# Hybrid encoder step on one core: the last output pair in another order, its last product in two column halves, a shorter 1/sqrt for one column, and the final gain multiplied in ahead

## The chip, the core and the metric

The kernel runs on one core of a Trainium2 chip. The metric is the time of one execution on the device in microseconds (us), lower is better. The engines work in parallel, each on its own list of instructions in order: PE (matrix products, with PEld for the load of the stationary operand), DVE and ACT (elementwise work), POOL (a few copies and DMA issues) and SP (DMA issues). They wait for each other by semaphores. DMA queues are named after the engine that issues (SPq, ACTq, POOLq).

## The reference

One layer on 4096 prompt rows and 32 sample rows of width 1024. What this case touches is the end of it: the output projection, the residual and the last RMSNorm.

```python
def rmsnorm(x, g):
    xf = x.astype(jnp.float32)
    y = xf * lax.rsqrt(jnp.mean(xf * xf, axis=-1, keepdims=True) + EPS)
    return (y * g.astype(jnp.float32)).astype(x.dtype)
...
    h = rmsnorm(x, norm_g)
    proj = jnp.einsum('btd,de->bte', h, w_in)
    u, v, z_a, xb, z_b = jnp.split(proj, ...)
    a = u * chunk_mlp(layernorm(v, ln_v_g, ln_v_b), w_spatial, b_spatial) * jax.nn.silu(z_a)
    b = pool_mix(x_ext, pos0, w_pool, pool_scale) * jax.nn.silu(z_b)
    y = x + jnp.einsum('bte,ed->btd', jnp.concatenate([a, b], axis=-1), w_out)
...
y_prompt = rmsnorm(xp, final_g)
```

`concat(a, b)` is 2048 wide, `w_out` is 2048 x 1024, `final_g` has 1024 entries.

## The kernel before

All large products are made in float32 precision from two parts: each operand is split in a high part (rounded to the type that PE multiplies fast) and the rest, and each product is high x high, high x low and low x high, so three matmuls per 128 rows of the contraction. On top of that the products are blocked 2 x 2 by a scheme with seven products instead of eight (numbers `q` 0 to 6), whose operands are sums and differences of blocks.

The output projection works on pairs of row tiles: `OutPair(z, i)` takes rows 256 i to 256 i + 255 (tiles n = 0 and 1, 128 rows each) and one half z of the 2048 contraction rows. First all 16 pairs with z = 0 (their sums go to `part` in DRAM, or stay in SBUF for the last two), then those with z = 1, which finish the rows. The very last step of the program is pair 13 with z = 1.

One product is 4 x 3 matmuls of 128 x 128 by 128 x 512 into one PSUM bank (`multiply`, L671 to L680). Products share banks: 0, 2 and 4 one, 3 and 6 another, 1 and 5 have their own. After a product DVE adds the bank to halves of the two result tiles `y[0]`, `y[1]` (L684; which half after which product is the table in L681). Left half means columns 0 to 511. With z = 1, ACT squares each finished half and sums it over the columns into `ss` (L688, an ACTIVATE and an ACTIVATION_READ_ACCUMULATOR). Product 1 finishes the left half of tile 0, product 4 the right half of tile 1, product 5 the right half of tile 0, product 6 the left half of tile 1.

`finish` (L691) takes the two sums, divides by 1024 and adds EPS (L700, L701), makes 1/sqrt by a bit trick and three Newton steps (`rsqrt`, L82 to L91: two steps for the first guess, then three times three), multiplies the tile by that column and by the gain `f_bc` (L706, DVE) and stores it (L709). For all pairs but the last it runs after product 2 of the next pair, on both tiles, and stores over POOL's queue. In the last pair `finish(0)` is called right after product 5 and `finish(1)` after product 6 at the end of the program, each with its own 13 steps; there the scaling goes in two halves of 512 columns, and the left half is stored over SP's queue, the right one over ACT's.

The instructions of an engine are put in order by the recording layer when the program is built; `tc.keep_in_program_order` (used by the change) keeps an instruction behind those recorded before it on its engine.

Of the kernel before, what the change touches and what calls it, by code (L numbers as in the profile page):

```python
# [10 lines left out]
BF16 = mybir.dt.bfloat16  # L11
# [4 lines left out]
P = 128  # L16
D = 1024
# [18 lines left out]
def stream_step(ctx: ExitStack, tc, x_prompt, x_sample, state_pool, norm_g, w_in, ln_v_g, ln_v_b,  # L36
# [39 lines left out]
    def small(tag, n, rows=P):  # L76
        return smallp.tile([P, 8], F32, tag=tag, name=tag)[:rows, :n]
# [4 lines left out]
    def rsqrt(a, n, rows=P):  # L82

        y, t = small("rs_y", n, rows), small("rs_t", n, rows)
        nc.vector.tensor_single_scalar(t.bitcast(I32), a.bitcast(I32), 1, ALU.logical_shift_right)
        nc.vector.tensor_scalar(y.bitcast(I32), t.bitcast(I32), -1.0, float(0x5F3759DF), ALU.mult, ALU.add)
        for _ in range(3):
            nc.vector.tensor_tensor(t, y, y, ALU.mult)
            nc.vector.scalar_tensor_tensor(t, t, -0.5, a, ALU.mult, ALU.mult)
            nc.vector.scalar_tensor_tensor(y, t, 1.5, y, ALU.add, ALU.mult)  # L90
        return y  # L91

    def slot():
        return slots.tile([P, 2 * 4 * WIDE], F32R, tag="slot", name="slot")
# [525 lines left out]
    class OutPair:  # L620
# [39 lines left out]
        def begin(self, y=None):  # L660
# [7 lines left out]
                self.ss = smallp.tile([P, 2, 2], F32, tag="sq", name="sq", bufs=4)  # L668
            self.acc = {}

        def multiply(self, q):  # L671
            own = {0: 0, 1: 1, 2: 0, 3: 3, 4: 0, 5: 5, 6: 3}[q]
            if own == q:
                self.acc[own] = acc_tile()
            x, w = self.ops[q], w_slots[self.z, q]
            a, fresh = self.acc[own], own == q
            for k in range(4):
                mm(a, x[:, 0, k, :], w[:, k, 0], start=fresh and k == 0, stop=False, skip_group_check=True)  # L678
                mm(a, x[:, 0, k, :], w[:, k, 1], start=False, stop=False, skip_group_check=True)  # L679
                mm(a, x[:, 1, k, :], w[:, k, 0], start=False, stop=k == 3, skip_group_check=True)  # L680
            for n, h, bank in {0: [(0, 0, 0)], 1: [(0, 0, 1)], 2: [(1, 0, 0)], 3: [(1, 1, 3)], 4: [(0, 1, 0), (1, 1, 0)],  # L681
                               5: [(0, 1, 5)], 6: [(1, 0, 3)]}[q]:
                y = self.y[n][:, h * 512:(h + 1) * 512]
                nc.vector.tensor_tensor(y, self.acc[bank], y, ALU.add)  # L684
            if self.z and q in (1, 4, 5, 6):
                n, h = {1: (0, 0), 4: (1, 1), 5: (0, 1), 6: (1, 0)}[q]
                junk = sum_p.tile([P, 2 * 512], BF16, tag="sum", name="junk")[:, :512]
                nc.scalar.activation(junk, self.y[n][:, h * 512:(h + 1) * 512], AF.Square,  # L688
                                     accum_out=self.ss[:, n, h:h + 1])

        def finish(self, last=None):  # L691
            t0 = 2 * self.i * P
            if self.z == 0:
                for n in range(2):
                    nc.gpsimd.dma_start(part[t0 + n * P:t0 + (n + 1) * P, :], self.y[n])
                return
            tiles = (0, 1) if last is None else (last,)
            a = small("ssa", 2)
            ss, a = self.ss[:, tiles[0]:tiles[-1] + 1], a[:, :len(tiles)]
            nc.vector.tensor_tensor(a, ss[:, :, 0], ss[:, :, 1], ALU.add)  # L700
            nc.vector.tensor_scalar(a, a, 1.0 / D, EPS, ALU.mult, ALU.add)  # L701
            r = rsqrt(a, len(tiles))
            for n in tiles:
                y = self.y[n]
                for z, c in enumerate((slice(0, 512), slice(512, D)) if last is not None else (slice(0, D),)):
                    nc.vector.scalar_tensor_tensor(y[:, c], y[:, c], r[:, n - tiles[0]:n - tiles[0] + 1], f_bc[:, c],  # L706
                                                   ALU.mult, ALU.mult)
                    queue = nc.gpsimd if last is None else (nc.sync, nc.scalar)[z]
                    queue.dma_start(yp[t0 + n * P:t0 + (n + 1) * P, c], y[:, c])  # L709

    class OutSample:

# [49 lines left out]
    with ExitStack() as ph:  # L762
# [215 lines left out]
            groups += [pools[2:4]] + [[x] for x in gates + pools[4:]] + [pools[:2]]  # L978
        n_sets = len(groups)
        pairs = [[OutPair(z, i) for i in range(SEQ // (2 * P))] for z in range(2)]  # L980
        groups += [[x] for x in pairs[0][:-2]] + [pairs[0][-2:], pairs[1][-2:]] + [[x] for x in pairs[1][:-2]]
        orders = [[(g[0], q) for q in range(NQ)] if len(g) == 1 else lagged(*g) for g in groups]
        steps = [x for order in orders for x in order]
        first = {id(s): i for i, (s, q) in reversed(list(enumerate(steps))) if q == 0}
        loads = [(first[id(s)], 1, s) for g in groups for s in g]
# [78 lines left out]
    with ExitStack() as ph:  # L1064
        y_p = pool("y_p", 6, ph)
        spare_p = pool("spare_p", 2, ph)
        ps_more = pool("ps_more", 2, ph, space=bass.MemoryType.PSUM)

        def y_tile():
            return y_p.tile([P, D], F32, tag="y", name="y")  # L1070

        def more_tile():
            return ps_more.tile([P, 512], F32, tag="more", name="more")

        def spare_tile():
            return spare_p.tile([P, D], F32, tag="spare", name="spare")


        m_edge = DEC + HALO
        state = {}  # L1080

        def state_load(k):
            if k == 0:
                state["acc"] = [more_tile(), more_tile()]
            state["st"] = st = sum_p.tile([P, 512], F32R, tag="sum", name="st")[:, :P]
            nc.sync.dma_start(st.bitcast(F32), stk[:, k * P:(k + 1) * P])
            state["raw"] = raw = raw_tile()
            nc.sync.dma_start(raw, w_in[0, k * P:(k + 1) * P, 3 * D:4 * D])

        def state_split():  # L1090
            hi, lo = state["parts"] = [weight_tile().rearrange("p h k t -> p (h k t)") for _ in range(2)]
            nc.scalar.copy(hi, state["raw"])
            lo_part(lo, state["raw"], hi)

        def state_rows(k):
            accs, st, (hi, lo) = state["acc"], state["st"], state["parts"]
            for z in range(2):
                c = slice(z * 512, (z + 1) * 512)
                mm(accs[z], st, hi[:, c], start=k == 0, stop=False, skip_group_check=True)
                mm(accs[z][:m_edge], st[:, :m_edge], lo[:, c], start=False, stop=k == KT - 1, skip_group_check=True)  # L1100
            if k == KT - 1:
                low = raw_tile()
                for z in range(2):
                    c = slice(z * 512, (z + 1) * 512)
                    nc.scalar.copy(low[:m_edge, c], accs[z][64:64 + m_edge])
                    nc.vector.tensor_tensor(low[:m_edge, c], accs[z][:m_edge], low[:m_edge, c], ALU.add)
                nc.sync.dma_start(st_prompt[0, 0], low[m_edge - POOL_STATE:m_edge])
                nc.sync.dma_start(st_sample[0, 0], low[DEC - POOL_STATE:DEC])

        samples = {n_sets + 1: OutSample(0), len(groups) - 6: OutSample(1)}  # L1110
        kept, ended = [], None
        for n in range(n_sets, len(groups)):
            g, order = groups[n], orders[n]
            for s in g:
                s.begin(kept.pop(0) if kept else None)
            if g[0].z and ended is None:
                f_bc = spare_tile()
                nc.sync.dma_start(f_bc, final_g.partition_broadcast(P))
            for m, (s, q) in enumerate(order):
                at += 1  # L1120
                prepare(at + LEAD)
                if m == 0 and n in samples:
                    samples[n].load()
                k = n - n_sets - 4
                if 0 <= k < KT and m in (0, 2):
                    state_load(k) if m == 0 else state_split()
                s.multiply(q)
                if n == len(groups) - 1 and q == 5:
                    s.finish(0)
                if m == 2 and ended:  # L1130
                    for x in ended:
                        x.finish()
                if s is g[-1] and n + 1 < len(groups) and groups[n + 1][0].stage != s.stage:
                    load_out_weights(1, q)
                if 0 <= k < KT and m == 6:
                    state_rows(k)
            if n in samples:
                samples[n].multiply()
            ended = g
            if g[0].z == 0 and len(g) == 2:  # L1140
                kept, ended = [x.y for x in g], None
        ended[0].finish(1)


# [27 lines left out]
```

## Time and profile before

| | us |
|---|---|
| median of 3 runs | 2402.03 |
| the three runs | 2402.02, 2402.03, 2408.12 |
| the profiled execution, its own time | 2403.8 |
| its span in the profile | 2402.0 |
| PE busy | 2372.8 (99% of the span) |
| DVE busy | 1799.3 (75%) |
| ACT busy | 894.6 (37%) |

The span goes from the first to the last event that the profile shows. Rows of the timeline give start and duration in us, then engine, source line, operation, result and operands ("out<-in"), the shape in partitions x elements, a count where equal rows are merged, and in brackets the idle time of the engine ahead of it with what ended it. Operands are named by the program's tiles: `acc` and `more` are PSUM banks, `wop` split operands, `slot` the split weights, `spare` holds the gain, `sq` the sums of squares, `rs_t` and `rs_y` the columns of 1/sqrt, `ssa` its argument. Matmuls are pipelined, so that one starts before the one ahead has drained; their ends are modelled.

### The profile page before, as it was taken

What the parts mean: (1) busy time and instruction counts of PE and PEld (TensorE: products, weight loads), DVE (VectorE), ACT (ScalarE), POOL (GpSimd) and SP (SyncE); (2) the same over time, 40 slices, a digit from 0 to 9 for tenths busy, and PEclk for the clock granted to TensorE, in tenths of its full rate; (3) what the DMA queues carried; (4) which work ended last, traced back from release to release, by engine and by line L of the source; (5) the groups of instructions that cost most, each with busy time, mean ns of one, the idle gap of its engine ahead of it and who ended that gap; (6) DMA issues with size and microseconds to landing.
All of it is one profiled execution on the core that took longest, in us unless ns stands there. A gap on an engine that the chain in (4) does not pass through costs nothing.

```text
span 2402.0 us, 32539 instructions
## 1 busy us (share of the span) xinstructions
PE 2372.8 (99%) x11910; PEld 1987.7 (83%) x11910; DVE 1799.3 (75%) x3327; ACT 894.6 (37%) x1594; POOL 198.9 (8%) x386
## 2 busy tenths in 40 slices
PE   8999999999999999999999999999999999999998
PEld 6788887788888888888888899999978788888876
DVE  6977787866787766877668776668767777588887
ACT  5555544333433333333334333333323232233332
POOL 1000000100011000111000110112200000000000
PEclk9999999999999999999999999999999999999999
DMA  9878977422448334474334472334687776855442
GB/s 282 287 284 264 271 249 241 141 92 92 149 129 294 103 97 132 132 276 135 106 105 141 167 264 87 99 102 149 223 308 258 255 259 228 308 177 166 155 128 83
DMA packets 325241, 445.56 MB, mean 185 GB/s; under 512 B 19324, under 2 KB 248444, under 8 KB 322392
## 3 DMA queue, kind: packets, MB, share of 16 engines
q1 hardware_dynamic: 273336, 354.65, 44.8%
q0 software_dynamic: 21136, 69.29, 8.0%
q10 hardware_dynamic: 30608, 19.53, 2.9%
q8 instruction: 94, 1.54, 0.3%
q14 instruction: 67, 0.55, 0.1%
HBM read 273.75 MB, written 169.66 MB: 185 GB/s over the span
## 4 chain that ended last, share of the span: by engine, by line
PE 96%; DMA 1%; DVE 1%; ACT 0%; issue 0%; SPq 0%; DVEq 0%; ACTq 0%
PE acc L172 22%; PE acc L174 22%; PE acc L173 22%; PE acc L678 8%; PE acc L680 8%; PE acc L679 8%; PE sp L893 2%; PE tr L442 1%; PE acc L237 1%; DMA slot<-wops 1%; DMA wops<-raw 0%; DMA vt<-in_w_in_dram 0%; PE more L742 0%; PE more L741 0%; PE tr L373 0%; DVE slot L80 0%
## 5 line engine op out<-in xcount | busy, mean ns | idle before, releaser
L172 PE MATMUL acc<-slot,wop 128*128 128x512 f32 (+1 forms) x2240 | 791.9, 354 | 1.2 <-ACT t L148 1.2
L174 PE MATMUL acc<-slot,wop 128*128 128x512 f32 (+1 forms) x2240 | 784.4, 351 | 0.9 <-DVE wop L80 0.9
L173 PE MATMUL acc<-slot,wop 128*128 128x512 f32 (+1 forms) x2240 | 784.4, 350 | 0.0
L80 DVE TENSOR_TENSOR wop<-raw,wop 128x512 fp32r<-128x512 f32 x510 | 353.1, 695 | 160.2 <-ACT wop L105 140.6
L172 PEld LDWEIGHTS acc<-slot,wop 128*128 128x128 f32 x2240 | 422.5, 189 | 59.6 <-ACT t L148 1.7
L174 PEld LDWEIGHTS acc<-slot,wop 128*128 128x128 f32 x2240 | 421.7, 188 | 60.4 <-DVE wop L80 1.4
L173 PEld LDWEIGHTS acc<-slot,wop 128*128 128x128 f32 x2240 | 422.4, 189 | 57.1 <-issue 0.2
L105 ACT CAST wop<-raw 128x512 fp32r<-128x512 f32 x340 | 210.3, 621 | 404.2 <-PE acc L174 320.6
L678 PE MATMUL acc<-slot,wop 128*128 128x512 f32 x896 | 353.6, 395 | 4.7 <-DMA slot<-wops 3.6
L679 PE MATMUL acc<-slot,wop 128*128 128x512 f32 x896 | 353.5, 395 | 0.0
L680 PE MATMUL acc<-slot,wop 128*128 128x512 f32 x896 | 353.2, 395 | 0.0
L146 DVE TENSOR_TENSOR t<-acc,t 128x512 f32<-128x512 f32 (+1 forms) x320 | 186.6, 584 | 128.6 <-ACT t L155 72.0
L684 DVE TENSOR_TENSOR y<-acc,y 128x512 f32<-128x512 f32 x256 | 173.3, 687 | 99.4 <-PE acc L680 98.0
L678 PEld LDWEIGHTS acc<-slot,wop 128*128 128x128 f32 x896 | 168.7, 188 | 45.6 <-issue 4.0
L680 PEld LDWEIGHTS acc<-slot,wop 128*128 128x128 f32 x896 | 168.8, 188 | 39.7
L679 PEld LDWEIGHTS acc<-slot,wop 128*128 128x128 f32 x896 | 168.8, 188 | 39.2
L172 PE MATMUL acc<-slot,op 128*128 128x512 f32 x448 | 181.0, 405 | 0.0
L174 PE MATMUL acc<-slot,op 128*128 128x512 f32 x448 | 177.1, 396 | 0.0
L173 PE MATMUL acc<-slot,op 128*128 128x512 f32 x448 | 176.8, 395 | 0.0
L640 ACT CAST wop<-raw 128x512 fp32r<-128x512 f32 x160 | 98.1, 620 | 190.1 <-PE acc L680 178.6
L80 DVE TENSOR_TENSOR wop<-sum,wop 128x512 fp32r<-128x512 f32 x200 | 137.0, 685 | 29.0 <-ACT wop L105 23.6
L912 POOL DMA_DIRECT2D abT<-t x128 | 69.5, 543 | 871.7 <-DVE t L924 631.8
(203 smaller groups left out, 2488.8 us busy)
## 6 DMA issues: line engine op xcount, KB each, us to landing
raw<-in_w_in_dram SPq DMA_DIRECT2D x102, 512.0 KB, 4.1
xops<-op SPq DMA_DIRECT2D x72, 512.0 KB, 5.9
abT<-t POOLq DMA_DIRECT2D x128, 256.0 KB, 3.6
raw<-abT SPq DMA_DIRECT2D x64, 512.0 KB, 5.2
slot<-xops SPq DMA_DIRECT2D x30, 1024.0 KB, 10.8
slot<-wops SPq DMA_DIRECT2D x14, 2048.0 KB, 9.1
xt<-in_x_prompt_dram SPq DMA_DIRECT2D x32, 512.0 KB, 4.9
raw<-v_all SPq DMA_DIRECT2D x32, 512.0 KB, 3.5
```

Of the source, the lines that this page charges most:

```text
L80: nc.vector.tensor_tensor(out, src, hi.bitcast(F32), ALU.subtract)
L105: nc.scalar.copy(hi, src)
L146: add = lambda o, x, y: nc.vector.tensor_tensor(o, x, y, ALU.add)
L172: mm(acc, sh, mh, start=fresh and k == 0, stop=False, skip_group_check=True)
L173: mm(acc, sh, ml, start=False, stop=False, skip_group_check=True)
L174: mm(acc, sl, mh, start=False, stop=k == 3, skip_group_check=True)
L640: nc.scalar.copy(t[:, 0], src)
L678: mm(a, x[:, 0, k, :], w[:, k, 0], start=fresh and k == 0, stop=False, skip_group_check=True)
L679: mm(a, x[:, 0, k, :], w[:, k, 1], start=False, stop=False, skip_group_check=True)
L680: mm(a, x[:, 1, k, :], w[:, k, 0], start=False, stop=k == 3, skip_group_check=True)
L684: nc.vector.tensor_tensor(y, self.acc[bank], y, ALU.add)
L912: nc.gpsimd.dma_start(abT[row, :, t0:t0 + HALF], t[:, :HALF])
```

## The change

The last pair gets a class of its own, `LastPair`, with its products in the order 0, 1, 2, 3, 4, 6, 5. Product 6, now last but one, finishes tile 1. Product 5, now last, is made in two halves of 256 columns, each in a bank of its own (`more`), with an add and a square of its own.

Tile 1 is multiplied by the gain into a tile `out` as soon as its halves are finished, and so is the left half of tile 0 in place; the squares are taken before that. What is left at the end is a multiplication by the column 1/sqrt: for tile 1 one copy on ACT with a scale, 1024 wide, and one store over SP's queue; for tile 0 one copy on ACT (left half, stored over ACT's queue) and one multiplication by column and gain on DVE (right half, stored over SP's).

The 1/sqrt works on m = -(sum/1024 + EPS)/2, into which the sums are added as they come, one step each. A Newton step is then two instructions instead of three: t = y * y * m, y = (t + 1.5) * y. The constant of the first guess is changed to fit m. `finish` loses its argument and its branch for single tiles.

```diff
+    def rsqrt_steps(m):
+        y, t = small("rs_y", 1), small("rs_t", 1)
+        stt = nc.vector.scalar_tensor_tensor
+        guess = [lambda: nc.vector.tensor_single_scalar(t.bitcast(I32), m.bitcast(I32), 1, ALU.logical_shift_right),
+                 lambda: nc.vector.tensor_scalar(y.bitcast(I32), t.bitcast(I32), -1.0, float(0x9EF759DF), ALU.mult,
+                                                 ALU.add)]
+        return y, guess + 3 * [lambda: stt(t, y, y, m, ALU.mult, ALU.mult),
+                               lambda: stt(y, t, 1.5, y, ALU.add, ALU.mult)]
...
+        def product(self, q, acc, c, fresh=True):
+            x, w = self.ops[q], w_slots[self.z, q]
+            for k in range(4):
+                mm(acc, x[:, 0, k, :], w[:, k, 0, c], start=fresh and k == 0, stop=False, skip_group_check=True)
+                mm(acc, x[:, 0, k, :], w[:, k, 1, c], start=False, stop=False, skip_group_check=True)
+                mm(acc, x[:, 1, k, :], w[:, k, 0, c], start=False, stop=k == 3, skip_group_check=True)
...
+    class LastPair(OutPair):
+        ORDER = (0, 1, 2, 3, 4, 6, 5)
+        def multiply(self, q):
...
+            elif q == 1:
...
+                acc = product_tile(acc_tile)
+                tt(y0[:, lo], acc, y0[:, lo], ALU.add)
+                square(y0[:, lo], ss[:, 0, 0:1])
+            elif q == 4:
+                self.product(q, self.acc[0], lo, False)
+                for y in (y1, y0):
+                    tt(y[:, hi], self.acc[0], y[:, hi], ALU.add)
+                square(y1[:, hi], ss[:, 1, 1:2])
+                tt(y0[:, lo], y0[:, lo], f_bc[:, lo], ALU.mult)
+                tt(self.out[:, hi], y1[:, hi], f_bc[:, hi], ALU.mult)
+                for n in range(2):
+                    ts(self.m[n], ss[:, n, n:n + 1], scale, shift, ALU.mult, ALU.add)
+            elif q == 6:
+                self.product(q, self.acc[3], lo, False)
+                in_order(tt(y1[:, lo], self.acc[3], y1[:, lo], ALU.add))
+                square(y1[:, lo], ss[:, 1, 0:1])
+                in_order(tt(self.out[:, lo], y1[:, lo], f_bc[:, lo], ALU.mult))
+            else:
+                (m0, m1), t0 = self.m, 2 * self.i * P
+                sums = [ss[:, 0, 1:2], small("end2", 1)]
+                r1, steps = rsqrt_steps(m1)
+                steps.insert(0, lambda: stt(m1, ss[:, 1, 0:1], scale, m1, ALU.mult, ALU.add))
+                for n, acc_sum in enumerate(sums):
+                    c = slice(n * 256, (n + 1) * 256)
+                    acc = product_tile(more_tile, c)
+                    c = slice(512 + n * 256, 512 + (n + 1) * 256)
+                    in_order(tt(y0[:, c], acc, y0[:, c], ALU.add))
+                    square(y0[:, c], acc_sum)
+                    for _ in range(6 if n == 0 else 3):
+                        in_order(steps.pop(0)())
+                nc.scalar.activation(self.out, self.out, AF.Copy, scale=r1)
+                nc.sync.dma_start(yp[t0 + P:t0 + 2 * P, :], self.out)
+                for acc_sum in sums:
+                    in_order(stt(m0, acc_sum, scale, m0, ALU.mult, ALU.add))
+                r0, steps = rsqrt_steps(m0)
+                for step in steps:
+                    in_order(step())
+                nc.scalar.activation(y0[:, lo], y0[:, lo], AF.Copy, scale=r0)
+                stt(y0[:, hi], y0[:, hi], r0, f_bc[:, hi], ALU.mult, ALU.mult)
+                nc.sync.dma_start(yp[t0:t0 + P, hi], y0[:, hi])
+                nc.scalar.dma_start(yp[t0:t0 + P, lo], y0[:, lo])
...
+        pairs[1][-3] = LastPair(1, SEQ // (2 * P) - 3)
...
-                if n == len(groups) - 1 and q == 5:
-                    s.finish(0)
...
-        ended[0].finish(1)
```

The order of the instructions shows three places; in the rows below 20522 is `y[0]` and 20523 is `y[1]` of the last pair, and `end0`, `end1`, `end2` are the new columns for m. On DVE, from the add of product 1 to those of product 4, before:

```order
L684 TENSOR_TENSOR y_20522<-acc_20548,y_20522 128x512
L684 TENSOR_TENSOR y_20523<-acc_20531,y_20523 128x512
L684 TENSOR_TENSOR y_20523<-acc_20597,y_20523 128x512
L684 TENSOR_TENSOR y_20522<-acc_20531,y_20522 128x512
L684 TENSOR_TENSOR y_20523<-acc_20531,y_20523 128x512
```

and in the changed kernel, at the same place on DVE:

```order
L746 TENSOR_TENSOR y_20522<-acc_20551,y_20522 128x512
L753 TENSOR_TENSOR y_20522<-y_20522,spare_18079 128x512
L698 TENSOR_TENSOR y_20523<-acc_20530,y_20523 128x512
L756 TENSOR_SCALAR end0_20548<-sq_20526 128x1
L698 TENSOR_TENSOR y_20523<-acc_20600,y_20523 128x512
L751 TENSOR_TENSOR y_20523<-acc_20530,y_20523 128x512
L751 TENSOR_TENSOR y_20522<-acc_20530,y_20522 128x512
L754 TENSOR_TENSOR raw_20550<-y_20523,spare_18079 128x512
```

The multiplication by the gain (L753), written under product 4, stands ahead of the add of product 2, and one step on a sum (L756) ahead of that of product 3.

At the end of the program DVE has, before, from the last add on (`ssa` and the rows below it belong to tile 1):

```order
L684 TENSOR_TENSOR y_20523<-acc_20597,y_20523 128x512
L89 SCALAR_TENSOR_TENSOR rs_t_20647<-rs_t_20647,ssa_20643 128x1
L90 SCALAR_TENSOR_TENSOR rs_y_20646<-rs_t_20647,rs_y_20646 128x1
L88 TENSOR_TENSOR rs_t_20647<-rs_y_20646 128x1
L89 SCALAR_TENSOR_TENSOR rs_t_20647<-rs_t_20647,ssa_20643 128x1
L90 SCALAR_TENSOR_TENSOR rs_y_20646<-rs_t_20647,rs_y_20646 128x1
L706 SCALAR_TENSOR_TENSOR y_20522<-y_20522,rs_y_20646,spare_18079 128x512 x2
L700 TENSOR_TENSOR ssa_20678<-sq_20526 128x1
L701 TENSOR_SCALAR ssa_20678<-ssa_20678 128x1
```

and in the changed kernel, from the last step of tile 1's 1/sqrt on, the third row behind the last add:

```order
L102 SCALAR_TENSOR_TENSOR rs_y_20651<-rs_t_20652,rs_y_20651 128x1
L778 SCALAR_TENSOR_TENSOR end0_20548<-sq_20526,end0_20548 128x1
L778 SCALAR_TENSOR_TENSOR end0_20548<-end2_20650,end0_20548 128x1
L98 TENSOR_SCALAR rs_t_20699<-end0_20548 128x1
L99 TENSOR_SCALAR rs_y_20698<-rs_t_20699 128x1
L101 SCALAR_TENSOR_TENSOR rs_t_20699<-rs_y_20698,end0_20548 128x1
L102 SCALAR_TENSOR_TENSOR rs_y_20698<-rs_t_20699,rs_y_20698 128x1
L101 SCALAR_TENSOR_TENSOR rs_t_20699<-rs_y_20698,end0_20548 128x1
L102 SCALAR_TENSOR_TENSOR rs_y_20698<-rs_t_20699,rs_y_20698 128x1
L101 SCALAR_TENSOR_TENSOR rs_t_20699<-rs_y_20698,end0_20548 128x1
L102 SCALAR_TENSOR_TENSOR rs_y_20698<-rs_t_20699,rs_y_20698 128x1
L783 SCALAR_TENSOR_TENSOR y_20522<-y_20522,rs_y_20698,spare_18079 128x512
```

Between the last add and the last scaling there were, before, 5 steps, 2 scalings and 13 steps; now there are 3 steps, 2 steps on the sums and 8 steps, and one scaling is left.

On ACT the last rows are, before:

```order
L688 ACTIVATE junk_20562,sq_20526<-y_20522 128x512
L688 ACTIVATE junk_20625,sq_20526<-y_20523 128x512
L688 ACTIVATE junk_20641,sq_20526<-y_20522 128x512
L688 ACTIVATE junk_20676,sq_20526<-y_20523 128x512
L709 DMA out_0_dram<-y_20522 128x512
L709 DMA out_0_dram<-y_20523 128x512
```

and in the changed kernel:

```order
L734 ACTIVATE junk_20628,sq_20526<-y_20523 128x512
L734 ACTIVATE junk_20647,sq_20526<-y_20523 128x512
L734 ACTIVATE junk_20667,sq_20526<-y_20522 128x256
L734 ACTIVATE junk_20689,end2_20650<-y_20522 128x256
L775 ACTIVATE raw_20550<-raw_20550,rs_y_20651 128x1024
L782 ACTIVATE y_20522<-y_20522,rs_y_20698 128x512
L785 DMA out_0_dram<-y_20522 128x512
```

The last square is split in two, and two scaled copies follow it, the 1024-wide one for tile 1 ahead of the one for tile 0.

More of the change, by code (lines that the diff above doesn't have):

```diff
@@ L674, in multiply @@
                 self.acc[own] = acc_tile()
[L675 to L680, printed above, removed]
+            self.product(q, self.acc[own], slice(0, 512), own == q)
             for n, h, bank in {0: [(0, 0, 0)], 1: [(0, 0, 1)], 2: [(1, 0, 0)], 3: [(1, 1, 3)], 4: [(0, 1, 0), (1, 1, 0)],
@@ L689, in multiply, with finish @@
                                      accum_out=self.ss[:, n, h:h + 1])
-        def finish(self, last=None):
+        def finish(self):
             t0 = 2 * self.i * P
@@ L696, in finish @@
                 return
-            tiles = (0, 1) if last is None else (last,)
             a = small("ssa", 2)
-            ss, a = self.ss[:, tiles[0]:tiles[-1] + 1], a[:, :len(tiles)]
-            nc.vector.tensor_tensor(a, ss[:, :, 0], ss[:, :, 1], ALU.add)
+            nc.vector.tensor_tensor(a, self.ss[:, :, 0], self.ss[:, :, 1], ALU.add)
             nc.vector.tensor_scalar(a, a, 1.0 / D, EPS, ALU.mult, ALU.add)
-            r = rsqrt(a, len(tiles))
-            for n in tiles:
+            r = rsqrt(a, 2)
@@ L704, in finish @@
+            for n in range(2):
                 y = self.y[n]
[L705 to L709, printed above, removed]
+                nc.vector.scalar_tensor_tensor(y, y, r[:, n:n + 1], f_bc, ALU.mult, ALU.mult)
+                nc.gpsimd.dma_start(yp[t0 + n * P:t0 + (n + 1) * P, :], y)
@@ new lines, in stream_step, with square, product_tile @@
+    class LastPair(OutPair):
+        ORDER = (0, 1, 2, 3, 4, 6, 5)
+        def multiply(self, q):
+            tt, stt, ts = nc.vector.tensor_tensor, nc.vector.scalar_tensor_tensor, nc.vector.tensor_scalar
+            scale, shift, ss = -0.5 / D, -0.5 * EPS, self.ss
+            lo, hi = slice(0, 512), slice(512, D)
+            y0, y1 = self.y
+            in_order = tc.keep_in_program_order
+            def square(y, acc):
+                junk = sum_p.tile([P, 2 * 512], BF16, tag="sum", name="junk")[:, :y.shape[1]]
+                nc.scalar.activation(junk, y, AF.Square, accum_out=acc)
+            def product_tile(tile, c=lo):
+                acc = tile()[:, :c.stop - c.start]
+                self.product(q, acc, c)
+                return acc
+            if q in (0, 2, 3):
+                OutPair.multiply(self, q)
+            elif q == 1:
+                self.m, self.out = [small(f"end{n}", 1) for n in range(2)], raw_tile()
+                acc = product_tile(acc_tile)
[8 more added lines that the diff above has]
+                tt(self.out[:, hi], y1[:, hi], f_bc[:, hi], ALU.mult)
+                for n in range(2):
+                    ts(self.m[n], ss[:, n, n:n + 1], scale, shift, ALU.mult, ALU.add)
[28 more added lines that the diff above has]
+                nc.scalar.dma_start(yp[t0:t0 + P, lo], y0[:, lo])
@@ L980, in stream_step @@
         pairs = [[OutPair(z, i) for i in range(SEQ // (2 * P))] for z in range(2)]
+        pairs[1][-3] = LastPair(1, SEQ // (2 * P) - 3)
         groups += [[x] for x in pairs[0][:-2]] + [pairs[0][-2:], pairs[1][-2:]] + [[x] for x in pairs[1][:-2]]
         orders = [[(g[0], q) for q in range(NQ)] if len(g) == 1 else lagged(*g) for g in groups]
+        orders[-1] = [(groups[-1][0], q) for q in LastPair.ORDER]
         steps = [x for order in orders for x in order]
```

## The prediction

> **What bounds the kernel now.** I read the page first (span, chain of waits), then each engine's timeline of the last 25 us, because the change touches only the last of 32 output steps (16 pairs, two halves of the contraction).
>
> ```profile
> span 2402.0 us, 32539 instructions
> ...
> PE 96%; DMA 1%; DVE 1%; ACT 0%; issue 0%; SPq 0%; DVEq 0%; ACTq 0%
> ```
>
> PE's matrix products fill 96% of the chain. On every engine the instructions ahead of the last pair stand as before, so what can change is the stretch around and behind the last products. PE's timeline dates it:
>
> ```profile
> 2388.61 0.39 PE L680 MATMUL acc<-slot,wop 128*128 128x512 f32 x1
> ...
> 2391.40 0.40 PE L680 MATMUL acc<-slot,wop 128*128 128x512 f32 x1
> ```
>
> These are the last matmuls of the last two of the pair's seven products. They start 2.79 us apart, the length of one product (12 matmuls, 0.2325 apart); the last ends at 2391.80. From there to the end of the span are 10.2 us. DVE's timeline shows most of them:
>
> ```profile
> 2380.67 0.69 DVE L684 TENSOR_TENSOR y<-acc,y 128x512 f32<-128x512 f32 x1 [0.66 <-PE acc L680]
> 2383.47 0.69 DVE L684 TENSOR_TENSOR y<-acc,y 128x512 f32<-128x512 f32 x1 [2.10 <-PE acc L680]
> 2386.25 1.29 DVE L684 TENSOR_TENSOR y<-acc,y 128x512 f32<-128x512 f32 x2 [2.09 <-PE acc L680]
> 2389.03 0.69 DVE L684 TENSOR_TENSOR y<-acc,y 128x512 f32<-128x512 f32 x1 [1.50 <-PE acc L680]
> ...
> 2392.00 0.68 DVE L684 TENSOR_TENSOR y<-acc,y 128x512 f32<-128x512 f32 x1
> ...
> 2393.56 1.41 DVE L706 SCALAR_TENSOR_TENSOR y<-y,rs_y,spare 128x512 f32<-128x512 f32 x2
> 2394.89 0.15 DVE L700 TENSOR_TENSOR ssa<-sq 128x1 f32<-128x1 f32 x1
> ...
> 2397.38 1.41 DVE L706 SCALAR_TENSOR_TENSOR y<-y,rs_y,spare 128x512 f32<-128x512 f32 x2
> ```
>
> The last add runs at 2392.00. DVE then finishes tile 0 (its two scalings at 2393.56) and only at 2394.89 starts the 13 one-column steps of tile 1: 2397.38 - 2394.89 = 2.49 us, 0.192 each. The last scaling ends at 2398.79. The stores of that tile follow; below are the two issues (timeline of the DMA queues), the landing times (DMA issues of the last 60 us: count, KB each, median us to landing) and three windows of 1 us (their last two numbers are the DMA share and GB/s):
>
> ```profile
> 2398.16 0.34 SPq L709 DMA_DIRECT2D out_dram<-y  x1
> 2398.83 0.36 ACTq L709 DMA_DIRECT2D out_dram<-y  x1
> ```
>
> ```profile
> y<-part SPq DMA_DIRECT2D x2, 512.0 KB, 3.7
> out_dram<-y SPq DMA_DIRECT2D x2, 256.0 KB, 2.0
> out_dram<-y ACTq DMA_DIRECT2D x2, 256.0 KB, 2.1
> ```
>
> ```profile
> 2398.00:2399.00 1.00, 0.00 (x0) 0.00 (x0) 0.79 (x2) 0.00 (x0) 0.00 (x0) 0.50 0.01 2
> 2399.00:2400.00 1.00, 0.00 (x0) 0.00 (x0) 0.00 (x0) 0.00 (x0) 0.00 (x0) 0.50 0.98 369
> 2400.00:2401.00 1.00, 0.00 (x0) 0.00 (x0) 0.00 (x0) 0.00 (x0) 0.00 (x0) 0.50 0.40 154
> ```
>
> So data starts 0.84 us after an issue starts, the two stores together need 0.98 + 0.40, about 1.40 us, at 369 GB/s, the last lands at 2398.83 + 2.1 = 2400.93, about 0.5 after its data, and 1.07 us of closing remain.
>
> **The change part by part.**
>
> *Products in halves.* The full product before the end (now number 6) still ends at 2389.00. Product 5 becomes 24 matmuls of 256 columns. Before has none of that width in this type; its nearest have 264 (PE's timeline in the last token block):
>
> ```profile
> 1599.72 0.29 PE L173 MATMUL acc<-slot,wop 128*128 128x264 f32 x1
> ...
> 1602.39 0.29 PE L174 MATMUL acc<-slot,wop 128*128 128x264 f32 x1
> ```
>
> Twenty-two steps in 2.67 us are 0.121 each; scaled to 256 columns 0.118. I take 0.119: the first half starts at 2388.84 and its twelfth matmul ends at 2388.84 + 11 x 0.119 + 0.28 = 2390.43; the second half ends at 2388.84 + 23 x 0.119 + 0.28 = 2391.86 (0.118 to 0.121: 2391.83 to 2391.90). PE pays 0.06 us.
>
> *Work pulled under the products.* Three 512-wide multiplications by g and a few one-column steps go between the adds. One place adds a wait: the multiplication of y0's left half (L753) now stands on DVE ahead of product 2's add and waits for ACT's square of that half. ACT's timeline of before:
>
> ```profile
> 2380.10 0.63 ACT L688 ACTIVATE junk<-y 128x512 bf16<-128x512 f32 x1 [6.28 <-issue]
> ...
> 2389.82 0.63 ACT L688 ACTIVATE junk<-y 128x512 bf16<-128x512 f32 x1 [1.48 <-DVE y L684]
> 2390.36 0.19 ACT L688 ACTIVATION_READ_ACCUMULATOR junk<-y 128x1 f32 x1
> ```
>
> That square ends 0.73 us after 2380.10, at 2380.83. The multiplication follows, the add moves from 2380.67 to about 2381.46 and ends at 2382.15. Behind it waits product 4, which adds into the bank that this add reads; product 3 ends at 2383.45, so over 1 us of cover stays. The other insertions end before 2389.03 or lie between 2389.63 and 2390.32, ahead of the first half's add. Cost nothing; without that cover each us would be a us of PE.
>
> *The chain behind the last product.* A 256-wide add from PSUM and a 256-wide square are not in the trace; the 264-wide ones are (groups by form, mean ns second after the bar):
>
> ```profile
> L146 DVE TENSOR_TENSOR t<-acc,t 128x264 f32<-128x264 f32 x128 | 54.5, 428 | 38.3 <-PE acc L174 25.6 <-ACT t L155 11.4
> ```
>
> ```profile
> L288 ACT ACTIVATE vt<-vt,nb,rs_y 128x1024 f32<-128x1024 f32 x32 | 38.1, 1237 | 34.9 <-DVE nb L286 34.9
> ...
> L1092 ACT CAST wop<-raw 128x1024 fp32r<-128x1024 f32 x8 | 8.4, 1050 | 12.3 <-PE acc L680 7.2 <-issue 5.1
> L878 ACT ACTIVATE t<-t 128x264 f32<-128x264 f32 x16 | 6.7, 422 | 8.3 <-DVE t L146 8.3
> ```
>
> Add: 2391.88 to 2392.31. Square: starts 0.10 later, as at 2389.82; it is 0.63 - 0.42 = 0.21 shorter than the 0.73 there: 2392.41 to 2392.93. Tile 1's chain of steps has by then all but ended: its sum is there at 2390.55, six steps run from 2390.78, three behind the add, r1 at 2392.76. Tile 0's first sum step is ready too, so 9 steps remain (one sum step, 2 for the guess, 3 x 2), at 0.192 = 1.73 us: 2392.96 to 2394.69. Against before, 13 steps at 2394.89 start 1.93 earlier and take 0.76 less. DVE scales y0's right half from 2394.69; the SP issue comes 0.78 behind a scaling's start (2397.38 to 2398.16), at 2395.47. ACT scales the left half from 2394.77; the 1024-wide copy ahead of it on ACT is over by 2394.19 (below), 0.5 us before r0. Each queue holds only these stores.
>
> A copy by a per-partition scale on ACT is not in the trace. 1024 wide it lies between the plain cast (1.05) and the activation with two such operands (1.24); 512 wide between 0.63 and 0.63 + 0.19 = 0.82. It has one operand, so I take the middle, 1.14 and 0.72, and keep the ends: the left half is issued at 2395.52 (2395.43 to 2395.62). [...]
>
> *Stores.* Tile 1 leaves as one 512 KB store: scaled from 2392.95 to 2394.09 (2394.00 to 2394.19), issued at 2394.12, data from 2394.96 for 1.40 to 2396.36. The last two issues, at 2395.47 and 2395.52, would start data at 2396.31: 0.05 behind the first store, at most 0.15. Both 256 KB stores now start together, so 1.40 us lie wholly behind the issue; before, most of the first had moved by the time the second began. Data ends at 2397.76, lands at 2398.25, span ends at 2399.32: 2.65 us less than 2402.0 (terms: 1.93 + 0.76 + 0.6 for scaling side by side, minus about 0.65 for the stores).
>
> [...]
>
> **Against the median.** The profiled execution took 2403.8 us around its span of 2402.0; the median of the three runs is 2402.03. Taking 2.65 off gives 2401.2 for the one and **2399.4 us** for the other, 0.11% less, where about 0.3% is what a measurement of this kernel can tell from no change.
>
> **The rivals.**
>
> *Stores collide, 2400.5.* The 512 KB store is on SP's queue just ahead of y0's right half. The loads of that size above took 3.7 us to land, 1.0 more than the 0.84 + 1.40 + 0.5 used here; if the store is that slow, or the ACT copy twice as long, the last two queue behind it for 1.0 to 1.2 us. Against it: 369 GB/s above, with nothing else moving.
>
> *Halves cost whole products, 2402.1.* The trace has 256-wide matmuls of another kind (plain f32 weights, PE timeline):
>
> ```profile
> 40.21 3.72 PE L237 MATMUL acc<-op,h 128*128 128x256 f32 x16
> ```
>
> There 16 take 3.72 us, 0.223 apart, as long as 512 columns here. At up to 0.2325 the product grows by 2.7 us and the gain is gone. Against it: the 264-wide row has the same operand type as the new halves.
>
> *Slower: a stall of the loads, 2405.5.* The third run took 2408.12, 6.1 more than the median. The list of waits shows where PE depends on transfers that the change doesn't touch:
>
> ```profile
> PE tr L373 <- DMA vt<-in_w_in_dram: 8.2, 2, 4.7
> ```
>
> If those first loads are 6.1 us later in the median run, 2399.4 becomes 2405.5; from 2.65 us on it is slower than before. For it: one run in three. Against: two runs agree to 0.01. The profile doesn't show which run stalled where.
>
> *The change doesn't do what it says*, r1 not being early: excluded by the order of DVE, where r1's steps stand ahead of the last sums.
>
> **How the numbers follow.** Forecast 78%: 2399.4, own terms give 2399.1 to 2399.9, and up to 1.8 more for runs like the profiled one. Stores 10%, whole-cost halves 4%, stall 8%. Leaving out the stall and the tails, the range is **2398.4 to 2402.6**. A gain over 0.3% would need 7.2 us out of a tail of 10.2: 1%. A loss over 0.3% needs more than the stall of the third run: 1%. Within 0.3%: 98%.
>
> **What would show it.** Right: 24 matmuls about 0.12 apart, the last ending near 2391.9; the last add 0.1 behind; r0's scaling about 2.8 us after that; ACT's 1024-wide copy at 1.13 or so, over before r0; the last stores issued within 0.1 us of each other near 2395.5; a span near 2399.3. Wrong: PE waiting before product 4, halves 0.2 apart, ACT's copy still running when r0 is ready, or stores landing over 3.3 us after their issue.

## The result and the profile after

| | us | runs |
|---|---|---|
| before, median | 2404.51 (2401.82 to 2408.12) | 12 |
| changed kernel, median | 2407.0 (2403.27 to 2410.57) | 12 |
| ratio after to before | 1.0016, 95% interval 1.0008 to 1.0023 | |
| changed kernel, the profiled execution: own time, span | 2406.89, 2405.1 | 1 |

The page of the changed kernel has, for its span and the chain that ended last:

```profile
span 2405.1 us, 32566 instructions
...
PE 97%; DMA 1%; DVE 1%; ACT 0%; SPq 0%; issue 0%; ACTq 0%; DVEq 0%
```

The changed kernel is 0.16% slower, where 0.11% faster was forecast; 2407.0 lies above the range of 2398.4 to 2402.6. The tail did what it was meant to do, though. PE's timeline of the changed kernel (start and duration in us) has the last full matmul and the first and the last of the halves:

```profile
2394.06 0.40 PE L688 MATMUL acc<-slot,wop 128*128 128x512 f32 x1
2394.30 0.28 PE L686 MATMUL more<-slot,wop 128*128 128x256 f32 x1
...
2396.91 0.28 PE L688 MATMUL more<-slot,wop 128*128 128x256 f32 x1
```

The last product but one starts its last matmul at 2394.06. Before, that was 2388.61. From there to the end of the span are 2405.1 - 2394.06 = 11.04 us, before 2402.0 - 2388.61 = 13.39: the tail is **2.35 us shorter**. But PE reaches the tail **5.45 us later**, although up to there it has as many instructions of the same kinds. The sum, +3.1, is the difference of the two spans. So the question of the experiments is what makes PE late.

DVE's timeline of the changed kernel shows the tail from the multiplication that waits (L753) on:

```profile
2386.24 0.69 DVE L753 TENSOR_TENSOR y<-y,spare 128x512 f32<-128x512 f32 x1 [0.84 <-ACT junk L734]
2386.85 0.68 DVE L698 TENSOR_TENSOR y<-acc,y 128x512 f32<-128x512 f32 x1
...
2388.90 0.69 DVE L698 TENSOR_TENSOR y<-acc,y 128x512 f32<-128x512 f32 x1 [1.30 <-PE acc L688]
...
2397.35 0.42 DVE L771 TENSOR_TENSOR y<-more,y 128x256 f32<-128x256 f32 x1
...
2398.46 0.16 DVE L778 SCALAR_TENSOR_TENSOR end<-end,end 128x1 f32<-128x1 f32 x1
...
2400.37 0.75 DVE L783 SCALAR_TENSOR_TENSOR y<-y,rs_y,spare 128x512 f32<-128x512 f32 x1
```

ACT's timeline has its two scaled copies and the issue of its store, the timeline of SP the other issue:

```profile
2398.32 1.15 ACT L775 ACTIVATE raw<-raw,rs_y 128x1024 f32<-128x1024 f32 x1
2400.42 0.72 ACT L782 ACTIVATE y<-y,rs_y 128x512 f32<-128x512 f32 x1 [0.95 <-DVE rs_y L102]
2401.17 0.39 ACTq L785 DMA_DIRECT2D out_dram<-y  x1
```

```profile
2401.15 0.34 SPq L784 DMA_DIRECT2D out_dram<-y  x1
```

The DMA issues (count, KB each, median us from issue to landing) give the landings:

```profile
out_dram<-raw SPq DMA_DIRECT2D x1, 512.0 KB, 2.6
out_dram<-y SPq DMA_DIRECT2D x1, 256.0 KB, 2.3
out_dram<-y ACTq DMA_DIRECT2D x1, 256.0 KB, 2.7
```

DVE waits 0.84 us for ACT's square, yet at 2388.90 it waits for PE again, so that wait costs PE nothing. The last two scalings start 0.05 apart, the last two stores are issued 0.02 apart, and the span ends 1.2 us behind the last landing (2401.17 + 2.7).

**Where PE is late.** The windows of a profile count the matmuls in a stretch of time. Below are two windows of 200 us, PE alone and only instructions that read `wop`, before and after: one of the mixing stage, one of the output stage. The number behind x is the count, the one behind it the granted clock.

```profile
1150.00:1350.00 200.00, 192.24 (x816) 1.00 0.37 116
2100.00:2300.00 200.00, 200.00 (x863) 1.00 0.49 157
```

```profile
1150.00:1350.00 200.00, 192.24 (x813) 1.00 0.38 119
2100.00:2300.00 200.00, 200.00 (x859) 1.00 0.48 155
```

PE is busy for the same 192.24 and 200.00 us at the same clock, and gets 3 and 4 matmuls fewer done, 0.4%. Nothing waits: **each 128 x 512 matmul takes a little longer**. Matmul by matmul, the time from the 10200th to the 11400th start, all in the output stage, is 278.85 us before (232.4 ns each) and 280.00 after (233.3); from the 5400th to the 6300th, in the mixing stage, 200.76 and 201.51. Between the 300th and the 9000th matmul the changed kernel loses 4.3 us, in the output stage 2.5; waits at the program's start (+1.5) and at the change of stage (-2.8) make up the rest. The longest wait at the change of stage is, in the lists of waits of before and after:

```profile
PE acc L678 <- DMA slot<-wops: 3.6, 1, 3.6
```

```profile
PE acc L686 <- DMA slot<-wops: 0.9, 1, 0.9
```

It differs as much between two profiles of the same kernel: from the 9000th to the 9300th matmul, around the change of stage, before takes 59.9 us, and the same kernel again (run e3 below) 57.1.

What differs ahead of the last pair, if not the instructions? The change adds three small tiles, `end0`, `end1` and `end2`, to the pool of small columns (`small`, L76): 3 x 2 buffers x 8 floats = 192 bytes in each partition. Every tile of a pool that is allocated behind it lies 192 bytes further on. The allocation of the two programs (byte at which the first buffer starts):

```
                                        before    after
slot  (moving operand, 7 x 16896)        17632    17632
raw   (6 x 4096)                        136800   136992
wop   (stationary operand, 7 x 4096)    161376   161568
wop minus slot, mod 256                    128       64
```

### The profile page after: what moved, and what is told of

Its sections match the earlier page's. It is cut to its first block, busy times and chain, and to the rows that moved or that the text cites. A ratio compares the mean times of both kernels' runs of the same rounds, so it can differ in the third digit from the quotient of the medians.

```text
span 2405.1 us, 32566 instructions
## 1 busy us (share of the span) xinstructions
PE 2379.4 (99%) x11922; PEld 1983.2 (82%) x11922; DVE 1797.7 (75%) x3323; ACT 895.4 (37%) x1598; POOL 191.7 (8%) x386
## 4 chain that ended last, share of the span: by engine, by line
PE 97%; DMA 1%; DVE 1%; ACT 0%; SPq 0%; issue 0%; ACTq 0%; DVEq 0%
PE acc L183 22%; PE acc L185 22%; PE acc L184 22%; PE acc L686 8%; PE acc L688 8%; PE acc L687 8%; PE sp L969 2%; PE tr L453 1%; PE acc L248 1%; DMA slot<-wops 0%; DMA wops<-raw 0%; DMA vt<-in_w_in_dram 0%; PE more L818 0%; PE more L817 0%; PE tr L384 0%; DVE slot L80 0%
## 6 DMA issues: line engine op xcount, KB each, us to landing
slot<-xops SPq DMA_DIRECT2D x30, 1024.0 KB, 10.7
```

## The experiments

Twelve further runs were made, each in five rounds beside the kernel before on the same chip; two of them repeat the kernels before and after. The spacings are the mean of the same 1200 matmuls of the output stage and, in brackets, the us from the 5400th to the 6300th. Distance is the start of the first `wop` minus that of the first `slot`, mod 256; the buffers of both lie multiples of 256 apart, and so do the parts of a buffer from which the matmuls of 128 x 128 by 128 x 512 read.

| run | distance | spacing, ns (us) | median, us | ratio to before, 95% |
|---|---|---|---|---|
| before | 128 | 232.4 (200.76) | | |
| after | 64 | 233.3 (201.51) | 2407.0 | 1.0016 (1.0008 to 1.0023) |
| e1 before + 192 B | 64 | 233.3 (201.51) | 2411.88 | 1.0029 (1.0018 to 1.0041) |
| e2 after, no new tiles | 128 | 233.3 (200.76) | 2398.96 | 0.9985 (0.9976 to 0.9994) |
| e3 before again | 128 | 232.4 (200.76) | 2403.51 | 1.0 (0.9991 to 1.0009) |
| e4 after again | 64 | 233.3 (201.51) | 2407.89 | 1.0015 (1.0006 to 1.0024) |
| e5 before, `wop` on + 192 | 64 | 233.3 (201.54) | 2407.6 | 1.0015 (1.0006 to 1.0024) |
| e6 before, behind `wop` + 192 | 128 | 233.3 (200.71) | 2406.23 | 1.001 (1.0002 to 1.0019) |
| e7 e2 + 64 B | 192 | 228.9 (197.97) | 2374.93 | 0.9885 (0.9867 to 0.9903) |
| e8 e2 + 128 B | 0 | 226.7 (196.11) | 2359.9 | 0.9816 (0.9803 to 0.983) |
| e9 before + 128 B | 0 | 226.7 (196.11) | 2359.51 | 0.9823 (0.981 to 0.9837) |
| e10 e2 + 160 B | 32 | 233.3 (201.55) | 2407.33 | 1.002 (1.0011 to 1.0029) |
| e11 e10, `slot` + 32 | 0 | 226.7 (196.11) | 2358.59 | 0.9814 (0.9801 to 0.9828) |
| e12 e2 - 128 B | 0 | 226.7 (196.60, with a wait of about 0.5) | 2359.77 | 0.9811 (0.9794 to 0.9828) |

### The 192 bytes without the change, and the change without them

e1 is the kernel before with one small tile widened:

```diff
-        return smallp.tile([P, 8], F32, tag=tag, name=tag)[:rows, :n]
+        return smallp.tile([P, 32 if tag == "nb" else 8], F32, tag=tag, name=tag)[:rows, :n]
```

> The kernel before, with one small tile enlarged so that every SBUF tile allocated behind the small ones (the split operands wop and op, raw, y, the gain) lies 192 bytes further on, as in the changed kernel; no instruction differs. The changed kernel's tail is shorter by 2.3 us but its products came 5.3 us later, with about 0.9 ns more from matmul to matmul in the output stage (0.2333 against 0.2324 us). Theory 'layout': the shift makes the matmuls slower; this kernel is about 5 us slower than before, its output-stage matmuls 0.2333 us apart. Theory 'executions differ': the matmul spacing varies from one execution or load of the program to the next, whatever the addresses; this kernel equals before within 1 us in the median, its spacing anywhere in 0.2324 to 0.2333. Theory 'new instructions': the 24 half matmuls and the new order slow PE throughout; equal to before, spacing 0.2324.

e2 is the changed kernel with its three columns in tiles that exist already, so that every address is that of before:

```diff
-                self.m, self.out = [small(f"end{n}", 1) for n in range(2)], raw_tile()
+                self.m, self.out = [small(("na", "ss")[n], 1) for n in range(2)], raw_tile()
...
-                sums = [ss[:, 0, 1:2], small("end2", 1)]
+                sums = [ss[:, 0, 1:2], small("nb", 1)]
```

> The changed kernel with its three new columns placed in small tiles that exist already, so that all SBUF addresses behind them are those of the kernel before; the instructions are the same. Layout: the loss goes and the shorter tail shows, 2.0 to 2.6 us faster than before (ratio about 0.999), spacing 0.2324. Executions differ: as before minus 2.3 in the median as well, but then the pad alone shows nothing. New instructions: still 2 to 3 us slower than before, spacing 0.2333.

e1 is slower by 0.29%, 7 us (4.3 to 9.9), where about 5 were expected, with not one instruction changed; its windows have 813 and 859 matmuls, as the changed kernel. e2 is faster than before by 0.15%, 3.6 us (1.4 to 5.8), and its mixing stage has the count of before again (windows of e2):

```profile
1150.00:1350.00 200.00, 192.23 (x817) 1.00 0.38 119
2100.00:2300.00 200.00, 200.00 (x859) 1.00 0.49 157
```

So the loss belongs to the position of the tiles and the gain to the last pair. In the output stage e2 has 859, not 863, and 233.3 ns where the layout theory expected 232.4: see e6.

Two controls on that chip, the kernels before and after once more, show how well such runs repeat:

> The kernel before, unchanged, as a control and for a second trace. Layout: ratio 1.000, spacing in the output stage 0.2324 as in the first trace. Executions differ: ratio 1.000 too, but the spacing of this trace may lie anywhere in 0.2324 to 0.2333.

> The changed kernel, unchanged, for a second trace and a second ratio on this chip. Layout: again 2 to 3 us slower than before, spacing 0.2333. Executions differ: the ratio may fall on either side of 1, and the spacing of this trace need not be 0.2333.

Both came out as they had: 1.0 and 1.0015, spacings and windows as in the first profiles.

### Which tile it is

e5 and e6 put the 192 bytes at other places of the kernel before: ahead of `wop` but behind `raw`, and behind `wop`, where only `sum`, `t`, `y`, `spare` and `cn` move. Both keep the place of all else (one small tile moves into the padding, another grows by as much). The lines of e5; in e6 the pool stands ahead of `sum_p`:

```diff
+    pad_p = pool("pad_p", 1)
     op_p = pool("wop_p", 7)
...
-                ss = small("sss", 2, DEC)
+                ss = pad_p.tile([P, 48], F32, tag="sss", name="sss")[:DEC, :2]
```

> The kernel before with the same instructions; the 192 bytes lie between the raw tiles and the split operands, so that wop (the stationary operand of PE from the second stage on) and all tiles behind it move by 192 bytes, while the raw tiles and the first stage's tiles stay. Theory 'stationary address': the matmuls slow down from the second stage on as in the kernel with everything moved: 900 matmuls of the fourth token block take 201.51 us instead of 200.76, and the time is 6 to 8 us over before. Theory 'other engines' tiles' (elementwise work and DMA on raw, y, sum get in PE's way at the new addresses): between 200.76 and 201.51, if raw matters 200.76.

> The kernel before with the same instructions; the 192 bytes lie behind the split operands, so that only sum, the temporaries, y and the gain move, wop and raw stay. Stationary address: no change of the matmuls, 200.76 us, and the time of before within 1.5 us. Other engines' tiles: 201.51 or between, and some us over before.

With `wop` moved, the mixing stage slows as in the changed kernel (201.54 us for the 900 matmuls); with only the tiles behind it moved, it stays (200.71). `raw` and the small columns are out as a cause of this slower spacing. The times are less clear. e5 is 0.15% slower than before, 3.6 us where 6 to 8 were expected, and half of e1's 0.29%; the two intervals overlap. PE's last matmul starts 6.8 us later in e1's trace than in e5's, and 4.9 of these come at the program's start (1.6) and around the change of stage (3.3), where executions of one kernel differ too. So that `wop` carries the whole loss is shown for the spacing and not for the time.

e6 is still 0.10% slower than before, 2.4 us where at most 1.5 was expected, and its output stage has 233.3 ns at the place of `wop` that gave 232.4. Its 1200 spacings fall into two groups, around 229.5 and 237.5 ns; those of before lie at 228 to 233, with some 14% at 240 and 241. e2 shows the pattern of e6 with every tile where before has it. So in the output stage there are two patterns at distance 128, 1 ns apart. The place of the tiles does not choose between them: e2 has before's places and instructions in this stage, and both patterns. From the 9400th to the 9770th matmul it shows that of before (232.3 ns on average), from the 10200th to the 11400th that of e6, and from the 11600th on that of before again. What chooses was not found.

### How it depends on the place

e7 and e8 move the tiles of e2 by 64 and by 128 bytes. e7 has 16 where e8 has 24:

```diff
-        return smallp.tile([P, 8], F32, tag=tag, name=tag)[:rows, :n]
+        return smallp.tile([P, 24 if tag == "nb" else 8], F32, tag=tag, name=tag)[:rows, :n]
```

> The changed kernel, its columns in existing tiles, with 64 bytes added ahead of the tiles behind the small ones: wop begins at 32 beyond a multiple of 128 bytes, as in the changed kernel (192 more), where before it is 96. Theory 'position within 128 bytes': slow, 201.51 us per 900 matmuls, 6 us over the version without the 64 bytes. Theory 'position within 256 or 512 bytes': not told by the position within 128; fast or slow as 160 within 256 has it.

> The same with 128 bytes: wop begins at 96 beyond a multiple of 128 bytes, as before, but at 224 within 256 where before it is 96. Position within 128 bytes: fast, 200.76 us, and like the version without added bytes, about 4 us faster than before. Position within 256 bytes: slow like the changed kernel.

This was the surprise of the study: not slower, but **1.15 and 1.84% faster**, 28 and 44 us. The position within 128 bytes had e7 slow and e8 4 us faster, so it is out, and no theory had gains of this size. e9 puts the same 128 bytes, by the same line, into the kernel before, without the new last pair:

> The kernel before with one small tile widened from 8 to 24 floats (two buffers), so that everything allocated behind it lies 128 bytes further on; instructions as before, the change of the last pair is not in it. Theory (the position of the stationary operand sets the spacing of every 128x512 matmul, and the change of the last pair is worth about 0.15% by itself): the same 226.7 ns spacing in the output stage as in e8, ratio to before 0.983, about 2363 us, 3 to 4 us more than e8. Rival (the gain of e8 needs the changed last pair): ratio 1.00. Rival (e8's chip was a lucky one): ratio above 0.99.

It is as fast (2359.51), so the gain has nothing to do with the change; the 3 to 4 us by which it was to be slower than e8 do not show. e10 and e11 tell whether the place of `wop` counts by itself or relative to `slot`. Both have `wop` at 161536, a multiple of 256. e10 widens `nb` to 32 floats and gives `ssb` one buffer; e11 has e8's line, and moves `slot` and the small tiles by 32 bytes through a constant ahead of them:

```diff
-            a = small("ssb", 1, DEC)
+            a = smallp.tile([P, 8], F32, tag="ssb", name="ssb", bufs=1)[:DEC, :1]
...
-    lvg = const.tile([P, HEADS], F32, name="lvg")
+    lvg = const.tile([P, HEADS + 8], F32, name="lvg")[:, :HEADS]
```

> The changed kernel with its new columns in existing small tiles, and 160 bytes in front of the operands (one small tile 32 floats wide, another with one buffer instead of two), so that the stationary operand starts at 0 mod 256 and the moving operand stays at 224. So far: position 32: 233.3 ns, 96: 232.4, 160: 228.9, 224: 226.7. Theory A (the position relative to the moving operand counts; 0 apart 226.7, 64 apart 233.3, here 32 apart): between these, about 230 ns, ratio about 0.99. Theory B (the absolute position counts, in lines of 64 bytes, and an operand that starts on a line is cheaper): at or under 226.7 ns, ratio 0.98 or less. Theory C (the absolute position counts, in steps of 64 bytes, 0 and 32 alike): 233.3 ns, ratio 1.00.

> As e10, the stationary operand at 0 mod 256, but the moving operand is also shifted, from 224 to 0 mod 256, by 32 bytes in a constant ahead of it. Theory A (the position relative to the moving operand counts; here they are 0 apart, as in e8): 226.7 ns, ratio 0.98. Theories B and C (only the absolute position of the stationary operand counts): as e10, whatever that gives.

e10 is at 233.3 ns and 2407.33 us, e11 at 226.7 and 2358.59. Their windows in the output stage, e10 first:

```profile
2100.00:2300.00 200.00, 200.00 (x859) 1.00 0.48 156
```

```profile
2100.00:2300.00 200.00, 200.00 (x883) 1.00 0.49 155
```

With `wop` at one byte, 32 bytes under `slot` are worth 2%; and with `slot` at one byte (e8 and e10), 32 bytes under `wop` are. So neither place counts alone, and theories B and C fall. Theory A had e11 right and e10 wrong by 3 ns: the value at distance 32 does not lie between those at 0 and 64. e12 reaches distance 0 from the other side, at 256 mod 512, with less memory than before:

```diff
-                ss = small("sss", 2, DEC)
+                ss = small("ssa", 2, DEC)
...
-            a = small("ssb", 1, DEC)
+            a = small("na", 1, DEC)
```

> The changed kernel with its new columns in existing small tiles, and two more small tiles (sss, ssb) put into tags that exist already, so that everything behind the small tiles lies 128 bytes lower than before; the stationary operand starts 143616 bytes behind the moving one (before 143744, e8 and e11 143872, e10 143904). Theory (the distance between the two operands mod 256 sets the spacing; here it is 0, as in e8 and e11): 226.7 ns in the output stage, 2359 us, ratio 0.982. Rival (the period is 512 bytes; here 256 of 512, which no run has had): another spacing, anywhere from 226 to 234 ns, ratio 0.98 to 1.00. Rival (the more room in front, the faster, for another reason than the distance): slower than before, ratio over 1.00.

226.7 ns and 2359.77 us again. The windows of e12 have 842 and 883 matmuls where before has 816 and 863:

```profile
1150.00:1350.00 200.00, 193.34 (x842) 1.00 0.41 129
2100.00:2300.00 200.00, 200.00 (x883) 1.00 0.48 155
```

and the engine rows of its page, beside that of the changed kernel, show the same 11922 matmuls in 48 us less of PE time (busy us, share of the span, count):

```profile
span 2357.6 us, 32566 instructions
...
PE 2331.1 (99%) x11922; PEld 1983.0 (84%) x11922; DVE 1791.6 (76%) x3323; ACT 894.4 (38%) x1598; POOL 206.7 (9%) x386
```

```profile
PE 2379.4 (99%) x11922; PEld 1983.2 (82%) x11922; DVE 1797.7 (75%) x3323; ACT 895.4 (37%) x1598; POOL 191.7 (8%) x386
```

The load of the stationary operand (PEld) takes the same 1983 us in both: it is not the load that gets longer in its record, but the distance from one matmul to the next.

e11 and e9 ran on one chip at the same distance, with and without the new last pair: 2358.59 and 2359.51 us, too close to tell apart by their intervals. From the start of the last matmul to the end of the span their traces have 8.1 and 10.7 us, as the changed kernel (8.2) and before (10.6). The last pair's gain is the same there; the waits ahead of it vary by more.

## Why the prediction was wrong

**The step that failed** is the second sentence of the argument: "On every engine the instructions ahead of the last pair stand as before, so what can change is the stretch around and behind the last products." The instructions do stand as before; the conclusion is wrong, since the operands they read lie elsewhere. The 512-wide matmuls ahead of the last pair became 0.4% slower. In the two profiles this makes 4.3 + 2.5 = 6.8 us, and the waits take 1.3 of them back, so that PE is 5.45 us late; against the trace of e3 in place of before it is 3.2 + 3.8 = 7.0. e1 shows the loss alone, e2 the gain alone. In the ratios, 1.0016 and 0.9985, the 192 bytes cost 0.31%, 7.5 us, uncertain by about 3. Between the profiles of e2 and the changed kernel, which share the slower pattern over most of the output stage, PE's last matmul is 4.6 us apart (2392.28 and 2396.91).

**The base** was low as well: 2402.03 was the median of three runs, and twelve have 2404.51. Of the 7.6 us between forecast and result this is 2.5. And 0.3% was not the least that a measurement can tell: with 12 runs on each side the interval is 0.15% wide, and no change (1.0) lies outside it.

**The tail** was right in mechanism and nearly in size: 2.35 us instead of 2.65 (the prediction's own end of the span, 2399.32, gives 2.68). By its terms:

- *Halves.* The 24 matmuls start 2.61 us from first to last, 0.113 apart; forecast was 0.119. The halves cost PE nothing. That they cost as much as whole ones is out.
- *The added wait* (L753) was 0.84 us and was covered, as forecast.
- *The chain.* From the last add to the last scaling it took 2400.37 - 2397.35 = 3.02 us, forecast 2.81. The mis-sized term is the step t = y * y * m, which the forecast priced like the other one-column steps. The groups of instructions of the changed kernel show it (count, busy us, mean ns of one):

```profile
L101 DVE SCALAR_TENSOR_TENSOR rs_t<-rs_y,end 128x1 f32<-128x1 f32 x6 | 1.3, 219 | 0.2
...
L102 DVE SCALAR_TENSOR_TENSOR rs_y<-rs_t,rs_y 128x1 f32<-128x1 f32 x6 | 0.9, 157 | 0.2
```

  From the start of such a step to the next it was 0.255 us instead of 0.192, and three times 0.06 us are 0.19 of the 0.21.
- *The copies on ACT* took 1.15 and 0.72 us, forecast 1.14 and 0.72.
- *Add and square of 256 columns.* For the 2399.9 at the upper end of the forecast's own terms no run shows a term that would give it: the last add (L771) and the last square (L734, at 2397.86) took 0.42 us each, near the 264-wide rows of the forecast (0.428 and 0.422), where 512 columns took 0.69 and 0.63. The two adds took 0.43 and 0.42, more in all than one of 512 columns, but the first started at 2395.86, beside PE.
- *The stores.* The 512 KB store landed 2.6 us after its issue, forecast 2.74 (0.84 + 1.40 + 0.5); the last two in 2.3 and 2.7, and did not collide with it: from 2401.6 to 2402.0 the DMA share is 0.05 or less, and 0.93 and more on either side. Behind the last landing the span went on for 1.2 us, forecast 1.07; this and the chain make up nearly all that the tail fell short.

**The slower rival** had nearly the right time (2405.5) for the wrong reason. It put the loss on late loads at the start. Of the waits of the changed kernel, that row reads

```profile
PE tr L384 <- DMA vt<-in_w_in_dram: 9.9, 2, 5.1
```

against 8.2 before: 1.7 us, less than the tail gained, and the wait for `slot` at the change of stage is 2.7 shorter. e2 runs with the same loads and is faster. That no rival of the prediction had operands in another place is why its range was too narrow on the slow side.

## What to carry to other kernels

Instructions that stand as before do not make a stage take its time of before (here 232.4 ns from matmul to matmul became 233.3): compare where the operands lie too, since a few new bytes in an early pool (here 192) move all tiles behind it. To time an edit by itself, keep the addresses (reuse tiles, or give back what is added), and pad the kernel before by the same bytes as a control. Where one kind of matmul fills the span, shift one operand by 32 to 128 bytes against the other before tuning anything smaller: here that was worth 1.8% (e9, the kernel before with nothing but 128 bytes), the new tail 0.15%.

## What the runs showed of the hardware that was not expected

The spacing of matmuls of 128 x 128 by 128 x 512, at a granted clock of 1.00, depends on the distance between stationary and moving operand in SBUF mod 256: **226.7 ns at 0, 233.3 at 32, 233.3 at 64, 232.4 (or 233.3) at 128, 228.9 at 192**. It is the same at 0 and at 256 mod 512, and with both operands moved together (e8, e11). That the other distances repeat every 256 bytes was not tested, and no other distance was measured for these matmuls.

The stretch of 264-wide matmuls shows no such order in its length: 328.8 to 330.7 us from the 6300th to the 9000th matmul over all 14 traces, with e5 (distance 64) at the lower end and e10 (32) at the upper. There the parts of the moving operand lie 2112 bytes apart, 64 beyond a multiple of 256, so that each product meets four distances whatever the first is. Place by place within a product the spacings do differ: from the second to the third matmul of a product's first half the median is 116 ns in all four runs at distance 0, and 121 to 124 in the ten others.

The runs measure that the place of the operands matters, by 6.6 ns of 233 between the distances 0 and 64. Why, they don't show: that it lies in PE's reads of the two is only argued, from the fact that the distance of just these two operands decides.

A one-column step with two operands of one column beside its first (L101: y once more, and m) took 0.219 us, with one and a constant (L102) 0.157.
